# Norm handovers of a two-layer trunk formed in PSUM, squares on ScalarE, weight splits on GpSimd

## Chip, cores and metric

The kernel runs on one core of a Trainium2 chip, as one launch. The metric is the device time of that launch in microseconds (us), the median of several runs. Matmuls run on TensorE (PE in the profile; its weight loads are PEld), elementwise work on VectorE (DVE), ScalarE (ACT) and GpSimd (POOL). SP only issues transfers. SBUF is the working memory, PSUM the eight banks of 128 x 512 float32 into which matmuls write.

## What is computed

512 tokens of 1024 float32 channels pass through two layers. Each layer has a mixer and a feed-forward network, and each of the four sub-layers is normalised on both sides:

```python
def rms_norm(x, g):
    return x * lax.rsqrt(jnp.mean(x * x, axis=-1, keepdims=True) + 1e-6) * g

def swiglu_ffn(h, w_ffn_in, w_ffn_out):
    g, u = jnp.split(h @ w_ffn_in, 2, axis=-1)
    return (jax.nn.silu(g) * u) @ w_ffn_out

def conformer_conv_module(h, w_pw1, b_pw1, w_dw, b_dw, ln_g, ln_b, w_pw2, b_pw2):
    a, g = jnp.split(h @ w_pw1 + b_pw1, 2, axis=-1)
    u = a * jax.nn.sigmoid(g)
    u = causal_depthwise_conv(u, w_dw) + b_dw
    u = jax.nn.silu(layer_norm(u, ln_g, ln_b))
    return u @ w_pw2 + b_pw2

for layer in range(2):
    u = rms_norm(h, norm_mix_pre[layer])
    m = shortconv_fox_mixer(u, ...) if layer == 0 else conformer_conv_module(u, ...)
    h = h + rms_norm(m, norm_mix_post[layer])
    f = swiglu_ffn(rms_norm(h, norm_ffn_pre[layer]), ...)
    h = h + rms_norm(f, norm_ffn_post[layer])
```

The convolution module, with 31 taps, is the mixer of layer 1. The mixer of layer 0 joins a gated three-tap convolution and an eight-head causal attention with a forget-gate bias, and projects both back to 1024 channels. The feed-forward network is 2816 wide.

## The kernel before

**Layout.** Channels lie on the 128 partitions and tokens on the free axis, so the stream is eight tiles `hin[k]` of 128 x 512. Tokens are worked on in two halves of 256 (`HT`). Every float32 product is three matmul passes over operands split as v = H + L (H is v rounded to float32r, L = v - H): `mm3`, L188 to L193.

**Weights** come as one stream of 512 KB chunks in the order of use (`ensure`, L154 to L176). SP's queue loads a chunk into one of two buffers `wr`, ScalarE copies it to H (L173), and one subtraction of 128 x 1024 makes L (L175). The strings `SPLIT1` to `SPLIT4` say which chunks' subtraction goes to GpSimd; all chunks of the feed-forward input matrix (`fi`) are on VectorE.

**Handovers.** Between two sub-layers stands a handover, called a crossing (`cross`, L756). There are three: crossing 0 (attention to the feed-forward of layer 0, 236 to 290 us of the span), crossing 1 (to the convolution mixer, 615 to 685) and crossing 2 (to the feed-forward of layer 1, 840 to 892). The end of the kernel is half of one (from 1234 us). The class `Boundary` does each in these steps, per token half:

- `evict` (L638): a finished 128 x 256 or x 512 product is squared (ScalarE, L241) and copied out (L651), or added to an earlier part (VectorE, L645). The squares are added up on GpSimd, the last of the eight on VectorE (L234).
- `post0`: TensorE sums the partitions with ones (L256, a PSUM tile of its own), and VectorE turns the sums into 1/sqrt by three Newton steps on columns of two values (L276 to L291) in SBUF.
- `post1` (L655): TensorE spreads the columns over all partitions (L298). Then for each of the eight channel tiles k, VectorE forms t = s[k] * gpost * spread (L663, SBUF, two buffers), adds it to `hin[k]` in place (L672), ScalarE makes the rounded X = gpre * h (L674), VectorE its rest (L675), and GpSimd squares h (L247) and adds the squares up (L234, the last one on VectorE).
- `pre0`, `pre1`: the same statistics for the norm ahead of the next product; the spread result is copied to R (L683), which scales the next product's outputs.

TensorE's order is the program's own (a manual schedule); the other engines' orders come from a scheduler, which also places every wait. In a crossing TensorE runs the last rows of the old product for half 1, then `quads`: four rows of the new product over one half, first its eight k with rounded X (a unit of 8 matmuls each), then its eight k with the rest (4 matmuls each). The statistics are inserted after so many units (`POST0`, `POST1`, `AP0`, `AP1`, `BP0`, `BP1`, `LATE0`, `LATE1`), so TensorE stops at an insertion whose inputs are late.

**The convolution mixer.** Each channel tile's u (`glu`, L957) goes through memory into four token phases (`phases_of`), its taps are spread into blocks (`bands_of`, L881, L878, on GpSimd, VectorE or ScalarE by `BUILD`), TensorE applies them, and VectorE does the remaining taps (L918). The parts of this that need no u (the split of the last tile's taps, `picks`, the load of `bands`) stand ahead of crossing 1 in the program, and each tile's blocks are built as soon as the scheduler finds room.

**End.** Without a next norm, `post1` forms t into two sets of SBUF tiles and adds it to `hin[k]` (L668; in half 1 four of the eight on GpSimd), and the output leaves by pairs of tiles (L670).

Of the kernel before, what the change touches and what calls it, by code (L numbers as in the profile page):

```python
# [59 lines left out]
POOL_POST = (0, 1, 3, 5)  # L60
# [4 lines left out]
SPLIT4 = 'PDPPPDDD'  # L65
PAD = TAPS - 1
# [5 lines left out]
# columns of the packed per-channel vectors  # L72
# [15 lines left out]
def trunk(tc, x, vec, bands, w_xa, w_in, w_v, w_f, w_out, w_fi, w_fo, w_p1, w_p2, out):  # L88
    """Feature-major trunk: channels on partitions, tokens on the free axis.

    Every float32 product is carried by three float32r passes over operands
    split as v = H + L (H: v rounded to float32r, L = v - H).
    """
# [7 lines left out]
    with tc.tile_pool(name="sb", bufs=1) as sb, tc.tile_pool(  # L101
# [15 lines left out]
        # ---- weights: one stream of 512 KB chunks, split into H and L ahead of use  # L117
# [31 lines left out]
        pool_split = {(n, i) for n, w in (("p1", SPLIT1), ("p2", SPLIT2), ("in", SPLIT3), ("out", SPLIT4)) for i, c in enumerate(w) if c == "P"}  # L149
# [4 lines left out]
        def ensure(n, pieces=1):  # L154
            """Load and split chunks up to number n; the first chunks after a norm have their own room."""
            while len(split) < min(n, len(chunks)):
# [12 lines left out]
                for i in range(pieces):  # L169
# [4 lines left out]
                    eng = nc.gpsimd if (name, count[name]) in pool_split else nc.vector  # L174
                    eng.tensor_tensor(out=l[:, cs], in0=raw[:, cs], in1=h[:, cs], op=ALU.subtract)  # L175
# [19 lines left out]
        # ---- constants  # L195
# [12 lines left out]
        # ---- per-token statistics: sums over channels as columns, one per block of 128 tokens  # L208
        class Sums:
            """Sums over channels of a list of channel tiles, per token half, as columns:  # L210
            the tiles are added up elementwise, then ones contract the partitions."""
# [12 lines left out]
            def room(self, hf, pool=False):  # L224
                if self.n[hf] == 0:
                    return self.acc[:, hf * HT : (hf + 1) * HT]
                return alloc("sqp" if pool else "sq", (P, HT), F32, 2)

            def put(self, hf, t, last, eng=None):
                """t: [128, 256], one channel tile of the half hf."""  # L230
                if self.n[hf]:
                    acc = self.acc[:, hf * HT : (hf + 1) * HT]
                    eng = nc.vector if last else eng or nc.gpsimd
                    eng.tensor_tensor(out=acc, in0=acc, in1=t, op=ALU.add)  # L234
# [4 lines left out]
            def square(self, hf, src, last, eng=None, **extra):  # L239
                t = self.room(hf)  # L240
                act(t, src, AF.Square, **extra)  # L241
                self.put(hf, t, last, eng)

            def square_pool(self, hf, src, last):
                """As square, off the scalar engine."""
                t = self.room(hf, True)
                nc.gpsimd.tensor_tensor(out=t, in0=src, in1=src, op=ALU.mult)  # L247
                self.put(hf, t, last)

            def cols(self, hf, tag="p"):  # L250
                ps = psum(tag, (P, 2))
# [7 lines left out]
        def weave(units, inserts=()):  # L259
            """Run a generator of tensor-engine work, calling each (n, f) of inserts after n units."""  # L260
# [11 lines left out]
        def newton(a, minus_half_a, n):  # L272
            """[128, n] columns a -> 1 / sqrt(a)."""
            y = alloc("st_y", (P, 4), F32, 3)[:, :n]
            u = alloc("st_u", (P, 4), F32, 3)[:, :n]
            ts(out=y.bitcast(I32), in0=a.bitcast(I32), scalar1=-0.5, scalar2=float(0x5F3759DF),  # L276
               op0=ALU.mult, op1=ALU.add)
            for _ in range(3):
                for j in range(n):
                    js = slice(j, j + 1)  # L280
                    stt(out=u[:, js], in0=y[:, js], scalar=minus_half_a[:, js], in1=y[:, js],  # L281
                        op0=ALU.mult, op1=ALU.mult)
                stt(out=y, in0=u, scalar=1.5, in1=y, op0=ALU.add, op1=ALU.mult)
            return y
# [580 lines left out]
        def bands_of(i):  # L865
# [3 lines left out]
            if i % 2:  # L869
                big = alloc("pth", (P, 2560), F32), alloc("ptl", (P, 2560), F32)  # L870
# [310 lines left out]
```

## Time and profile before

| | us |
|---|---|
| median of 3 runs (1251.49 to 1252.73) | 1251.75 |
| span of the profiled execution, first to last instruction | 1248.6 |
| TensorE busy in the span | 1185.8 (95%) |
| VectorE busy | 735.6 (59%) |
| ScalarE busy | 490.0 (39%) |
| GpSimd busy | 265.0 (21%) |
| mean granted TensorE clock | 0.978 of full speed |

The span is what the trace shows of one execution; that execution's own device time is not recorded beside it, so the median of the runs stands for it, and 3.15 us of it lie outside the span. "Busy" counts instructions of that engine only; a share over the whole span averages stages with different limits, so the stages are read one by one below.

### The profile page before, as it was taken

The numbers are of one execution on the slowest core, as the hardware profiler recorded it, in microseconds if no ns is written. First come the engines' busy times: TensorE is split into PE (matmuls) and PEld (weight loads), VectorE is DVE, ScalarE is ACT, GpSimd is POOL, SyncE is SP. The second block draws the span as 40 slices with busy tenths as digits, with TensorE's granted clock in tenths as the row PEclk, the third lists the DMA queues.
The fourth block names the chain that finished last, engine by engine and source line by source line (L and its number), as shares of the span: only waits on it lengthen the run. The fifth ranks groups of instructions, "written<-read, shape, count | busy, mean of one in ns | idle before, by whom it ended". The sixth has DMA issues, their size and how long they took to land.

```text
span 1248.6 us, 15995 instructions
## 1 busy us (share of the span) xinstructions
PE 1185.8 (95%) x6134; PEld 1005.8 (81%) x6134; DVE 735.6 (59%) x1266; ACT 490.0 (39%) x862; POOL 265.0 (21%) x268
## 2 busy tenths in 40 slices
PE   8899999989999999999988998898999999999996
PEld 6677677888888888888887897898888888888885
DVE  7578985496443234443398999948844422444425
ACT  4366664534332222332244575464332322332220
POOL 4132322460000000001475359124300000000021
PEclk9999999999999999999989999898999999999998
DMA  5332223313233233223221543123133233233212
GB/s 177 113 106 85 85 68 102 119 51 99 89 100 102 87 99 101 94 92 102 92 71 52 168 131 97 28 68 102 51 101 101 88 98 99 89 101 102 90 46 68
DMA packets 43116, 115.86 MB, mean 93 GB/s; under 512 B 4696, under 2 KB 14040, under 8 KB 43040
## 3 DMA queue, kind: packets, MB, share of 16 engines
q1 hardware_dynamic: 39936, 109.30, 28.1%
q10 hardware_dynamic: 2384, 3.15, 0.8%
q0 software_dynamic: 720, 2.39, 0.6%
q8 instruction: 48, 0.79, 0.3%
q14 instruction: 28, 0.23, 0.1%
HBM read 109.05 MB, written 5.78 MB: 92 GB/s over the span
## 4 chain that ended last, share of the span: by engine, by line
PE 73%; DVE 17%; DMA 4%; ACT 2%; issue 2%; POOL 1%; SPq 0%; ACTq 0%; DVEq 0%; POOLq 0%
PE pg L191 22%; PE pg L193 22%; PE pg L192 22%; DVE xl L675 2%; DVE h L672 2%; DVE wl L175 2%; DVE tb L663 2%; PE pg L737 1%; DVE st_u L281 1%; POOL acc L234 1%; PE ps L298 1%; PE pg L734 1%; DMA wr<-w_fi 1%; PE pg L735 1%; PE pp L541 1%
## 5 line engine op out<-in xcount | busy, mean ns | idle before, releaser
L191 PE MATMUL pg<-xh,wh 128*128 128x512 f32 (+1 forms) x960 | 372.1, 388 | 0.2 <-DVE z L459 0.2
L193 PE MATMUL pg<-xh,wl 128*128 128x512 f32 (+1 forms) x960 | 368.4, 384 | 2.0 <-DVE wl L175 2.0
L192 PE MATMUL pg<-xl,wh 128*128 128x512 f32 (+1 forms) x960 | 367.8, 383 | 2.0 <-DVE xl L331 2.0
L173 ACT ACTIVATE wh<-wr 128x1024 fp32r<-128x1024 f32 (+1 forms) x186 | 193.3, 1040 | 424.3 <-PE pg L192 349.9
L175 DVE TENSOR_TENSOR wl<-wr,wh 128x1024 fp32r<-128x1024 f32 (+1 forms) x157 | 192.3, 1226 | 168.2 <-ACT wh L173 168.1
L234 POOL TENSOR_TENSOR acc<-acc,sq 128x256 f32<-128x256 f32 x70 | 63.7, 925 | 749.5 <-ACT sq L241 746.5
L193 PEld LDWEIGHTS pg<-xh,wl 128*128 128x128 f32 x960 | 181.1, 189 | 38.8 <-DVE wl L175 3.0
L192 PEld LDWEIGHTS pg<-xl,wh 128*128 128x128 f32 x960 | 181.4, 189 | 36.6 <-DVE xl L331 2.8
L191 PEld LDWEIGHTS pg<-xh,wh 128*128 128x128 f32 x960 | 181.6, 189 | 33.9 <-issue 0.7
L191 PE MATMUL pg<-z,wh 128*128 128x512 f32 (+1 forms) x514 | 183.2, 357 | 0.0
L192 PE MATMUL pg<-z,wh 128*128 128x512 f32 (+1 forms) x514 | 182.1, 354 | 1.1 <-DVE z L391 1.1
L193 PE MATMUL pg<-z,wl 128*128 128x512 f32 (+1 forms) x514 | 182.1, 354 | 0.0
L192 PEld LDWEIGHTS pg<-z,wh 128*128 128x128 f32 x514 | 97.9, 190 | 15.9 <-DVE z L391 1.5
L191 PEld LDWEIGHTS pg<-z,wh 128*128 128x128 f32 x514 | 97.9, 190 | 14.7 <-ACT m L651 0.3
L193 PEld LDWEIGHTS pg<-z,wl 128*128 128x128 f32 x514 | 97.9, 190 | 14.4
L785 DVE TENSOR_TENSOR t<-pg,R 128x512 f32<-128x512 f32 (+1 forms) x48 | 31.0, 645 | 126.9 <-PE pg L193 126.7
L175 POOL TENSOR_TENSOR wl<-wr,wh 128x1024 fp32r<-128x1024 f32 x29 | 71.8, 2476 | 125.4 <-ACT wh L173 113.8
L783 DVE TENSOR_TENSOR t<-pg,R 128x512 f32<-128x512 f32 (+1 forms) x48 | 31.0, 646 | 86.7 <-PE pg L193 83.0
L918 DVE SCALAR_TENSOR_TENSOR ps<-z,vecs,ps 128x512 f32<-128x512 f32 x69 | 47.7, 747 | 0.1
L674 ACT ACTIVATE xh<-h,vecs 128x256 fp32r<-128x256 f32 x48 | 23.4, 506 | 58.4 <-DVE h L672 58.4
L734 PE MATMUL pg<-xh,wh 128*128 128x256 f32 x160 | 44.9, 305 | 1.2 <-ACT xh L1082 1.2
L735 PE MATMUL pg<-xh,wl 128*128 128x256 f32 x160 | 44.3, 301 | 0.0
(250 smaller groups left out, 1526.2 us busy)
## 6 DMA issues: line engine op xcount, KB each, us to landing
wr<-w_fi SPq DMA_DIRECT2D x88, 512.0 KB
wr<-w_fo SPq DMA_DIRECT2D x44, 512.0 KB
wr<-w_p SPq DMA_DIRECT2D x24, 512.0 KB
wr<-w_in SPq DMA_DIRECT2D x16, 512.0 KB
wr<-w_out SPq DMA_DIRECT2D x8, 512.0 KB
h<-x SPq DMA_DIRECT2D x8, 256.0 KB
wr<-w_xa SPq DMA_DIRECT2D x8, 256.0 KB
wr<-w_v SPq DMA_DIRECT2D x4, 512.0 KB
```

The costliest lines, as they stand in the source:

```text
L173: act(h[:, cs], raw[:, cs], AF.Copy)
L175: eng.tensor_tensor(out=l[:, cs], in0=raw[:, cs], in1=h[:, cs], op=ALU.subtract)
L191: mm(ps, wh, xh, start=first, stop=False)
L192: mm(ps, wh, xl, start=False, stop=False)
L193: mm(ps, wl, xh, start=False, stop=last)
L234: eng.tensor_tensor(out=acc, in0=acc, in1=t, op=ALU.add)
L663: stt(out=t, in0=self.s[k][:, cs], scalar=col(self.gpost + k), in1=rp, op0=ALU.mult, op1=ALU.mult)
L734: mm(ps, wh, xt[0][k][:, cs], start=k == 0 and m % 2 == 0, stop=False)
L735: mm(ps, wl, xt[0][k][:, cs], start=False, stop=False)
L783: tt(out=tg, in0=pg, in1=R[:, cs], op=ALU.mult)
L785: tt(out=tu, in0=pu, in1=R[:, cs], op=ALU.mult)
L918: stt(out=a if j < n - 1 else res, in0=u[:, j : j + T], scalar=w_col(i, j), in1=a, op0=ALU.mult, op1=ALU.add)
```

## The change

Two new PSUM uses are the core. A `Boundary` takes four PSUM banks for its whole life: bank 0 (tag p) for the columns, the Newton work and the spread of both halves, bank 1 (tag o) for t in its lower half and the last square in its upper half, banks 2 and 3 (tag s) for the new stream tile hp, two channel tiles to a bank. The stream tile is written back to `hin[k]` by ScalarE. The squares of the norm ahead move from GpSimd to ScalarE. The first eight `fi` chunks of each layer are split on GpSimd, and every GpSimd split is cut into pieces of 128 x 256. The preparation of the convolution's taps is queued, on each engine, behind the evaluation of the second `glu` tile. At the end all eight additions are on VectorE.

```diff
-POOL_POST = (0, 1, 3, 5)
+SPLIT5 = ('PPPPPPPP' + 'D' * 36) * 2
...
+        pool_split = {... ("out", SPLIT4), ("fi", SPLIT5)) ...}
...
-                    eng = nc.gpsimd if (name, count[name]) in pool_split else nc.vector
-                    eng.tensor_tensor(out=l[:, cs], in0=raw[:, cs], in1=h[:, cs], op=ALU.subtract)
+                    if (name, count[name]) not in pool_split:
+                        tt(out=l[:, cs], in0=raw[:, cs], in1=h[:, cs], op=ALU.subtract)
+                        continue
+                    for c in range(i * D // pieces, (i + 1) * D // pieces, HT):
+                        nc.gpsimd.tensor_tensor(out=l[:, c : c + HT], in0=raw[:, c : c + HT], in1=h[:, c : c + HT],
+                                                op=ALU.subtract)
...
+            def square(self, hf, src, last, eng=None, room=None, **extra):
+                t = self.room(hf) if room is None else room
                 act(t, src, AF.Square, **extra)
                 self.put(hf, t, last, eng)
-            def square_pool(self, hf, src, last):
...
+            for s in range(3):
+                for js in each_slice(n):
+                        ts(out=u[:, js], in0=y[:, js], scalar1=y[:, js], scalar2=minus_half_a[:, js],
+                           op0=ALU.mult, op1=ALU.mult)
+                for js in each_slice(n):
+                    ts(out=(res if s == 2 else y)[:, js], in0=u[:, js], scalar1=1.5, scalar2=y[:, js],
+                       op0=ALU.add, op1=ALU.mult)
...
+            def bank(self, i):
+                if self.banks is None:
+                    self.banks = [psum(t) for t in ("po" if self.gpre is None else "poss")]
+                return self.banks[i]
+            def half(self, hf):
+                return self.bank(0)[:, hf * HT : (hf + 1) * HT]
...
-                        self.sums.square(c // HT, src[...], m == NK - 1, **extra)
+                        self.sums.square(c // HT, src[...], m == NK - 1,
+                                         room=self.bank(1)[:, HT:] if m == NK - 1 else None, **extra)
...
+            def stats(self, sums, hf):
+                r = self.half(hf)
+                self.cols[hf] = rsqrt_cols(sums.cols(hf, ps=r[:, :2]), 2, 1.0 / D, RMS_EPS, r[:, 2:8])
...
-                rp = spread(*each(self.cols[hf], 2))[:, :HT]
+                rp = spread(*each(self.cols[hf], 2), ps=self.half(hf))
                 for k in range(NK):
-                    t = alloc("t", bufs=3)[:, :HT] if self.gpre is None and k % 2 else alloc("tb", (P, HT), F32, 2)
+                    t = self.bank(1)[:, :HT]
                     stt(out=t, in0=self.s[k][:, cs], scalar=col(self.gpost + k), in1=rp, op0=ALU.mult, op1=ALU.mult)
                     if self.gpre is None:
-                        eng = nc.gpsimd if hf and k in POOL_POST else nc.vector
-                        eng.tensor_tensor(out=o[:, k % 2], in0=hin[k][:, cs], in1=t, op=ALU.add)
+                        tt(out=o[:, k % 2], in0=hin[k][:, cs], in1=t, op=ALU.add)
                     else:
-                        tt(out=hin[k][:, cs], in0=hin[k][:, cs], in1=t, op=ALU.add)
-                        act(self.x[0][k][:, cs], hin[k][:, cs], AF.Copy, scale=g)
-                        stt(out=self.x[1][k][:, cs], in0=hin[k][:, cs], scalar=g, in1=self.x[0][k][:, cs], ...)
-                        self.pre.square_pool(hf, hin[k][:, cs], k == NK - 1)
+                        i = hf * NK + k
+                        hp = self.bank(2 + i // 2 % 2)[:, i % 2 * HT : (i % 2 + 1) * HT]
+                        tt(out=hp, in0=hin[k][:, cs], in1=t, op=ALU.add)
+                        act(self.x[0][k][:, cs], hp, AF.Copy, scale=g)
+                        stt(out=self.x[1][k][:, cs], in0=hp, scalar=g, in1=self.x[0][k][:, cs], ...)
+                        self.pre.square(hf, hp, k == NK - 1, room=self.bank(1)[:, HT:] if k == NK - 1 else None)
+                        act(hin[k][:, cs], hp, AF.Copy)
...
+        def prepare():
+            room = slot(16, (P, Q + 2 * LAST_TAPS), FR)
+            band = slot(17, (P, bands.shape[1]), F32)
+            nc.gpsimd.dma_start(band, bands)
+            act(wsh, wlast, AF.Copy)
+            nc.vector.tensor_reduce(out=picks, in_=ident.rearrange("p (q c) -> p c q", q=4), axis=AX.X, op=ALU.add)
+            tt(out=wsl, in0=wlast, in1=wsh, op=ALU.subtract)
...
-                if p < last:
+                if p == 0:
+                    return
+                if p == 1:
+                    with tc.issue_after(sig.ins), tc.issue_after(out.ins), tc.issue_after(bd.pre.ins):
+                        for i in range(2):
+                            phases_of(uu[i], i)
+                        prepare()
+                        for i in range(2):
+                            bands_of(i)
+                elif p < last:
                     phases_of(uu[p], p)
                     bands_of(p)
```

`bd.pre.ins` is GpSimd's last addition of squares of the norm ahead; `issue_after` fixes only the order of issue on that instruction's engine.

## Rows read from the trace of the kernel before

**Rows 1.** TensorE's own waits over the whole span: us in total, times, longest

```profile
PE pp L256 <- DVE acc L234: 12.2, 7, 3.3
PE ps L298 <- DVE st_y L283: 12.0, 8, 3.4
PE pg L734 <- ACT xh L674: 7.7, 11, 1.6
PE pp L541 <- DVE ptl L545: 4.2, 5, 1.5
PE po L560 <- DVE t L564: 1.6, 2, 1.0
```

**Rows 2.** Busy time by stretch: PE, PEld, DVE, ACT, POOL, clock, DMA share, GB/s

```profile
615.00:685.00 70.00, 57.87 (x382) 54.41 (x381) 61.67 (x122) 29.72 (x72) 45.36 (x50) 0.90 0.19 58
685.00:793.00 108.00, 102.61 (x641) 92.65 (x639) 104.79 (x154) 59.71 (x133) 64.97 (x57) 0.97 0.43 127
```

**Rows 3.** Timeline of the attention, 127 to 132 us: start, duration, [idle before]

```profile
126.90 2.74 POOL L175 TENSOR_TENSOR wl<-wr,wh 128x1024 fp32r<-128x1024 f32 x1 [8.37 <-ACT wh L173]
...
128.08 2.12 DVE L566 TENSOR_TENSOR z<-t,z 64x512 fp32r<-64x512 f32 x1
...
131.93 0.55 PE L541 MATMUL pp<-eye,h 128*128 128x128 f32 x3 [1.19 <-DVE ptl L545]
```

**Rows 4.** Single lines: duration ns min/median/max, first and last start, forms

```profile
L663 DVE SCALAR_TENSOR_TENSOR tb<-m,vecs,ps x56: 462/473/482, 245.1 to 1243.6; 128x256 f32<-128x256 f32 x56
...
L672 DVE TENSOR_TENSOR h<-h,tb x48: 406/562/961, 245.9 to 883.0; 128x256 f32<-128x256 f32 x48
...
L645 DVE TENSOR_TENSOR m<-pg,m x14: 416/691/692, 572.2 to 1226.1; 128x512 f32<-128x512 f32 x10, 128x256 f32<-128x256 f32 x4
...
L241 ACT ACTIVATE sq<-pg x22: 364/384/406, 225.2 to 1234.9; 128x256 f32<-128x256 f32 x22
...
L458 ACT ACTIVATE z<-pg,rcol x8: 467/476/502, 63.3 to 67.5; 128x256 fp32r<-128x256 f32 x8
...
L175 DVE TENSOR_TENSOR wl<-wr,wh x157: 672/1225/2581, 5.0 to 1205.5; 128x1024 fp32r<-128x1024 f32 x149, 128x512 fp32r<-128x512 f32 x8
```

**Rows 5.** Timeline, ScalarE and VectorE in turn on one PSUM bank, 64 to 65 us

```profile
64.22 0.87 DVE L459 SCALAR_TENSOR_TENSOR z<-pg,rcol,z 128x256 fp32r<-128x256 f32 x2
...
64.73 0.48 ACT L458 ACTIVATE z<-pg,rcol 128x256 fp32r<-128x256 f32 x1 [0.24 <-DVE z L459]
```

**Rows 6.** Timeline of crossing 1: a Newton step on VectorE and three of TensorE's waits

```profile
617.23 2.21 DVE L276 TENSOR_SCALAR st_y<-st_a 128x2 int32<-128x2 int32 x1
...
623.28 1.22 PE L298 MATMUL ps<-eye,st_y 128*128 128x128 f32 x4 [2.96 <-DVE st_y L283]
...
639.02 0.58 PE L256 MATMUL pp<-ones,acc 128*128 128x1 f32 x4 [3.28 <-DVE acc L234]
...
667.20 1.22 PE L298 MATMUL ps<-eye,st_y 128*128 128x128 f32 x4 [3.37 <-DVE st_y L283]
```

**Rows 7.** Timeline of crossings 0 and 2: loop starts, a weight copy, half 1's sums

```profile
245.13 0.86 DVE L663 SCALAR_TENSOR_TENSOR tb<-m,vecs,ps 128x256 f32<-128x256 f32 x2
...
253.77 1.04 ACT L173 ACTIVATE wh<-wr 128x1024 fp32r<-128x1024 f32 x1
...
257.67 0.58 PE L256 MATMUL pp<-ones,acc 128*128 128x1 f32 x4 [0.51 <-DVE acc L234]
...
851.39 0.87 DVE L663 SCALAR_TENSOR_TENSOR tb<-m,vecs,ps 128x256 f32<-128x256 f32 x2 [2.16 <-PE ps L298]
...
861.36 0.58 PE L256 MATMUL pp<-ones,acc 128*128 128x1 f32 x4 [1.55 <-DVE acc L234]
```

**Rows 8.** Timeline of the end, 1238 to 1245 us, VectorE

```profile
1238.17 0.35 DVE L281 SCALAR_TENSOR_TENSOR st_u<-st_y,st_b 128x1 f32<-128x1 f32 x2
...
1240.03 0.48 DVE L663 SCALAR_TENSOR_TENSOR tb<-m,vecs,ps 128x256 f32<-128x256 f32 x1 [1.32 <-PE ps L298]
...
1244.73 0.41 DVE L668 TENSOR_TENSOR xl<-h,t 128x256 f32<-128x256 f32 x1
```

More of the change, by code (lines that the diff above doesn't have):

```diff
@@ L148, in trunk @@
         count = {}
-        pool_split = {(n, i) for n, w in (("p1", SPLIT1), ("p2", SPLIT2), ("in", SPLIT3), ("out", SPLIT4)) for i, c in enumerate(w) if c == "P"}
+        pool_split = {(n, i) for n, w in (("p1", SPLIT1), ("p2", SPLIT2), ("in", SPLIT3), ("out", SPLIT4),
+                                              ("fi", SPLIT5)) for i, c in enumerate(w) if c == "P"}
         split = []
@@ L233, in put @@
                     eng = nc.vector if last else eng or nc.gpsimd
-                    eng.tensor_tensor(out=acc, in0=acc, in1=t, op=ALU.add)
+                    ins = eng.tensor_tensor(out=acc, in0=acc, in1=t, op=ALU.add).ins
+                    if not last:
+                        self.ins = ins
                 elif last:
@@ L237, in put, with cols @@
                 self.n[hf] += 1
-            def square(self, hf, src, last, eng=None, **extra):
-                t = self.room(hf)
+            def square(self, hf, src, last, eng=None, room=None, **extra):
+                t = self.room(hf) if room is None else room
                 act(t, src, AF.Square, **extra)
                 self.put(hf, t, last, eng)
-            def square_pool(self, hf, src, last):
[L246 to L251, printed above, removed]
+            def cols(self, hf, tag="p", ps=None):
+                if ps is None:
+                    ps = psum(tag, (P, 2))
                 a = self.only[hf]
@@ L291, in rsqrt_cols, with spread @@
             ts(out=b, in0=sums, scalar1=-0.5 * scale, scalar2=-0.5 * eps, op0=ALU.mult, op1=ALU.add)
-            return newton(a, b, n)
-        def spread(*cols, tag="s"):
-            ps = psum(tag)
+            return newton(a, b, n, room)
+        def spread(*cols, tag="s", ps=None):
+            if ps is None:
+                ps = psum(tag)
             for j, c in enumerate(cols):
@@ L634, in __init__ @@
                 self.cols = {}
+                self.banks = None
                 if gpre is not None:
@@ L965, in glu @@
             tt(out=tg, in0=pg, in1=R[:, cs], op=ALU.mult)
[L966 removed]
+            sig = act(tg, tg, AF.Sigmoid, bias=col(V_PW1 + 8 + p))
             tt(out=ta, in0=pa, in1=R[:, cs], op=ALU.mult)
[L968 to L969 removed]
+            out = stt(out=uu[p][:, PAD + c0 : PAD + c0 + cn], in0=ta, scalar=col(V_PW1 + p), in1=tg,
+                      op0=ALU.add, op1=ALU.mult)
             if c0 + cn == T:
[L971 removed]
+                if p == 0:
[8 more added lines that the diff above has]
+                elif p < last:
                     phases_of(uu[p], p)
```

65 lines of the change are left out of this document (33 added, 32 removed).

## Prediction, made before the changed kernel was run

> **What bounds the kernel now.** TensorE is busy for 95% of the span, so I first read its own waits, then where they lie, then what the engine named was doing. It stands for 1248.6 - 1185.8 = 62.8 us. The five largest groups of its waits make 37.7 of that, and 31.9 of these belong to the norm handovers [rows 1]: 12.2 us for VectorE's last addition of squares (L234), 12.0 for a Newton result (L283), 7.7 for X (L674). The attention adds 4.2 and 1.6. By stretch, crossing 1 is the worst: TensorE works 57.9 of 70 us, at a mean granted clock of 0.90, which is another 7 us of full speed lost [rows 2]. The convolution stretch is different: VectorE is busy 104.8 of 108 us there, so work added to VectorE is paid for.
>
> VectorE is late in the handovers because its operations with SBUF data stop while GpSimd runs. In the attention a GpSimd split occupies 126.90 to 129.64; a 64x512 VectorE operation issued at 128.08 lasts 2.12 us, until just behind the split's end, and TensorE then stands 1.19 us [rows 3]. In crossing 1 a Newton operation on two columns takes 2.21 us behind such a split, and TensorE waits 2.96 [rows 6]. Operations with a PSUM operand don't show this: L663 has 462 to 482 ns over all of its 56 runs, while L672, with SBUF alone, has 406 to 961 [rows 4].
>
> **The change, part by part.**
>
> *Splits in pieces.* A piece is a quarter of the 2.74 us split, so some 0.7 us (estimate). VectorE then waits at most that in place of up to 2.4. The five and two waits in the attention, 4.2 + 1.6 us, each follow such a hold [rows 1, 3]; I take **-4** (bounds 0 and -5.8). GpSimd's splits get dearer by some 0.3 us each for the three further starts; cover is its idle time.
>
> *Splits of eight `fi` chunks off VectorE.* In crossings 0 and 2 the last addition of half 0 stands behind a 1.23 us split on VectorE (L175 [rows 4]). Without it the loop starts some 0.9 us earlier in crossing 0 and 1.5 in crossing 2 (estimates: at most the split and its queueing, at least what of the 1.23 us lies behind the last square). Each queue position that GpSimd's pieces take delays its additions by up to 0.7; nobody waits for those until the eighth.
>
> *The loop over k.* Before, VectorE was the pace. Now three kinds of wait set it. t has one buffer, so product and sum alternate: 0.47 + 0.04 + 0.42 (L663, L645 [rows 4]) = 0.93 us to the first hp. And two engines that use one PSUM bank take turns even at different columns: ScalarE's copy of a bank's second half waited for VectorE's operation on its first half, whose data it does not need, and began 0.04 us behind it, at 64.73 [rows 5]. In the program's order hp of an odd k must wait for everything done with the even k in its bank: X 0.48 (as L458), rest 0.47, square and write-back 0.38 each (L241), the sum 0.42, four handoffs of 0.04: 2.3 us. A pair costs 2.3 + 0.9 = 3.2, eight tiles 0.9 + 3 x 3.2 + 2.3 = **12.9 us**. During half 0 ScalarE also has three weight copies of 1.04 [rows 7] and three evictions of 2 x 0.38, 5.4 us; its own chain work is 8 x 1.24 = 9.9 of the 12.9, so it has 3 us free, in bits. I let 1.1 of the 5.4 land in the chain: 14 us (bounds 12.9 and 18.3). VectorE has room: 8 x 1.2 us.
>
> *New links for TensorE.* Half 1's last square goes into bank 1, where t lives, so it waits for the whole loop of half 0; then 0.38 + 0.42 and handoffs: the sums of half 1 come 14.9 us behind the loop's start. Crossing 0: 245.13 - 0.9 + 14.9 = 259.1 in place of 257.67, +1.4. Crossing 2: 851.39 - 1.5 + 14.9 = 864.8 against 861.36, +3.4 [rows 7]. In half 1 `pre0` writes bank 0 while VectorE still reads the spread there; its last read is 12.9 - 2.3 = 10.6 us into the loop, and TensorE, four or five units of X in, arrives some 2 to 3 us earlier: +2.9 and +2.0. Against that, the waits for X that lie in these two crossings, up to 7.7 us [rows 1], are absorbed by the new ones. Together **+2** (bounds -7 and +11).
>
> *Crossing 1.* The Newton wait of 2.96 goes, TensorE spreads at 620.3, the loop starts at 620.9 and lasts 1 us more, since two splits stay on VectorE: sums of half 1 at 636.8 in place of 639.02, -2.2. The next Newton wait (part of the 12.0 of [rows 1]) is worth -1.8, the one at 667.20 -3.4 [rows 6], the new `pre0` wait +2, and of the 7 us lost to the clock [rows 2] two come back as the idle time shrinks: **-7.4** (bounds -12 and -2).
>
> *Newton columns in PSUM.* Each step has four single-column operations instead of two and one of two columns. A pair takes 0.35 [rows 8], so a step grows by some 0.2 and a Newton by 0.6. Cover is TensorE's units between the insertions, except at the end.
>
> *Tap preparation.* The `bands` load, the small copy and reduction, six GpSimd blocks, one ScalarE block and two VectorE blocks move behind the second `glu`, and the first tile's phase transfers on SP's queue, with the weights behind them, start about 1 us later. TensorE reaches the first taps some 14 us after, GpSimd's three blocks need 5. VectorE's share, some 3 us, falls into its full stretch [rows 2]: **+2** (0 to +4).
>
> *The end.* No cover here. The loop was 1240.03 to 1245.14 [rows 8] with four sums on GpSimd; one buffer of t makes it 8 x 0.85 = 6.9: +1.8. The last square waits for the loop of half 0, which also grows: +0.8. The Newton: +0.6. **+3.2** (2 to 4).
>
> Sum: -4 + 2 - 7.4 + 2 + 3.2 = -4.2 us, on a span of 1248.6: 1244.4. 3.15 us lie outside the span, so **1247.5** against the median of 1251.75 (-0.34%).
>
> *PSUM operands.* VectorE's operations of the loop now read PSUM where they read SBUF. A 128x256 sum with a PSUM operand takes 416 ns at least (L645), with SBUF alone 406 (L672) [rows 4]: 10 ns apart, so I charge nothing more. The Trainium skill (VectorE: DVE Perf Modes, section "The TRN2 errata — SBUF-src ops pay a fixed extra latency per instruction") says otherwise: its table gives an operation with a PSUM source a fixed part of 120 cycles and an SBUF one 58. By it every loop would be about 1 us longer; the two rows disagree with it.
>
> **The rivals.**
> *Slower: the handovers through the banks become the bound.* Place: half 0's loop, ScalarE's queue. If its fixed order puts the weight copies and evictions into the turns, the loop takes 17 us instead of 14, and the sums of half 1 come 3 us later in three crossings: -4.2 + 9 = +4.8, **1256.5**. It decides from 15.4 us per loop on. For it: ScalarE would be busy 15 of those us. Against: VectorE and GpSimd stop holding each other up. Chance 0.25. A dearer PSUM operand gives much the same: if each costs what lies between L672's fastest run and L663's median, 473 - 406 = 67 ns [rows 4], then with four VectorE operations of a pair on the chain a loop grows by 16 x 0.067 = 1.1 us; six loops 6.4, the end 1.1: +7.5 on the forecast, **1255.0**. L645's 416 speaks against it: 0.03. The errata table named above would act in this way.
> *Much faster: the banks don't hold anyone up* and VectorE's 1.2 us per k is the pace. Loops of 10 us: 3 to 4 us off each crossing's half 0 and the 2 to 3 of the `pre0` wait, together some -17 with part caught elsewhere, -12: **1235.5**. Against it stand [rows 5]. Chance 0.13.
> *No change:* the attention's waits stay, because the fixed order of VectorE and not the hold is what makes them late: -4.2 + 4 = **1251.5**. For it: pieces hold VectorE four times. Chance 0.14.
>
> **How the numbers follow.** The forecast's own case has 0.45 and reaches from 1240 to 1252, 0.33 of it faster by over 0.2% (2.5 us, about what a measurement of this kernel can tell from no change) and 0.12 within. Faster: 0.33 + 0.13 + 0.04 of the third rival = 0.50. Within 0.2%: 0.12 + 0.05 of the first + 0.08 = 0.25. Slower: 0.20 + 0.03 + 0.02 = 0.25. The range 1238 to 1256 leaves out most of the fast rival and the upper half of the slow one, about 0.2; the likeliest case's own range is 1240 to 1252.
>
> **What would show it.** Right: no VectorE operation over 1 us in the three crossings, the waits at L298 in crossing 1 gone, TensorE's waits at the sums of half 1 and at `pre0` longer than before, L672's successor in pairs some 3.2 us apart, an end later by 3 us. Wrong: X of neighbouring k less than 1.3 us apart throughout (the fast rival), half 0 loops above 15.4 us (the slow one), or attention waits as before.

## The result and the profile after

The changed kernel takes **1288.57 us** (median of 4 runs, 1287.27 to 1289.27) against 1252.24 for the kernel before, run beside it: a ratio of 1.0285 (95% interval 1.0271 to 1.0300), 36 us slower. The forecast was 1247.5, its range 1238 to 1256. The profiled execution has a span of 1287.5 us.

The page's busy times, after:

```profile
PE 1190.8 (92%) x6134; PEld 1009.6 (78%) x6134; DVE 700.6 (54%) x1296; ACT 518.1 (40%) x958; POOL 291.7 (23%) x373
```

TensorE is busy 5 us longer, at a mean granted clock of 0.964 instead of 0.978, and idle for 96.7 us instead of 62.8. VectorE has lost 35 us of work; it was not what was short. TensorE's own waits (us in total, times, longest):

```profile
PE pp L258 <- DVE acc L239: 29.9, 6, 11.0
PE pp L315 <- DVE st_y L298: 9.6, 5, 4.1
PE pp L258 <- DVE po L696: 8.8, 3, 4.0
PE pg L770 <- ACT m L680: 8.4, 1, 8.4
PE pg L770 <- ACT xh L708: 7.7, 11, 1.3
```

Against [rows 1], the wait for the last addition of squares has grown from 12.2 to 29.9 us with fewer cases. Two groups are new: TensorE's sums wait for `po`, which is the product of the loop that reads the spread (L696), and the first unit of the new product waits 8.4 us for an *eviction* (`m`, L680). The waits for X are the same 7.7 us, eleven times. The Newton wait has become smaller, not small. The attention's groups (L541, L560 before) are down to three cases of 0.3 us. TensorE also waits 3.8 us for GpSimd at taps of the convolution (770.15 us), where it did not wait before.

Both traces hold the same 6134 matmuls in the same order, so the same one can be read in both. Where it starts, and by how much the changed kernel lags:

| matmul | before | after | lag |
|---|---|---|---|
| last wait of the attention gone | 188.46 | 184.08 | -4.4 |
| first unit of crossing 0 | 252.73 | 258.13 | +5.4 |
| last spread of crossing 0 | 293.29 | 305.04 | +11.8 |
| sums of half 1, crossing 1 | 639.02 | 654.51 | +15.5 |
| last spread of crossing 1 | 680.90 | 695.22 | +14.3 |
| ahead of crossing 2 | 837.49 | 854.58 | +17.1 |
| sums of half 1, crossing 2 | 861.36 | 889.25 | +27.9 |
| last spread of crossing 2 | 897.73 | 929.44 | +31.7 |
| last spread of the end | 1238.77 | 1274.93 | +36.2 |
| end of the span | 1248.6 | 1287.5 | +38.9 |

A negative lag means that the changed kernel is ahead. Differences between the lags at the ends of the stretches give the account: attention -4.4, crossing 0 +16.2, crossing 1 +2.5, convolution +2.8, crossing 2 +14.6, end +7.2.

One pair of channel tiles of the loop, from the timeline of crossing 0 after:

```profile
245.46 0.43 DVE L706 TENSOR_TENSOR ps<-h,po 128x256 f32<-128x256 f32 x1
...
245.92 0.48 ACT L708 ACTIVATE xh<-ps,vecs 128x256 fp32r<-128x256 f32 x1 [0.17 <-DVE ps L706]
...
246.58 0.48 DVE L709 SCALAR_TENSOR_TENSOR xl<-ps,vecs,xh 128x256 fp32r<-128x256 f32 x1
...
247.15 0.38 ACT L248 ACTIVATE sq<-ps 128x256 f32<-128x256 f32 x1
247.43 0.38 ACT L712 ACTIVATE h<-ps 128x256 f32<-128x256 f32 x1
...
247.84 0.43 DVE L706 TENSOR_TENSOR ps<-h,po 128x256 f32<-128x256 f32 x1 [0.79 <-ACT h L712]
...
248.83 0.43 DVE L706 TENSOR_TENSOR ps<-h,po 128x256 f32<-128x256 f32 x1
```

Sum, X, rest, square and write-back of an even tile follow one another, and only then may the odd tile's sum enter the bank, 2.38 us later; with the 0.99 to the next bank a pair takes 3.37. In the loops of half 1 a pair takes more, 1.37 + 2.50 = 3.87 from sum to sum, because there VectorE forms the rest of the odd tile (277.19) ahead of the next bank's sum:

```profile
276.21 0.43 DVE L706 TENSOR_TENSOR ps<-h,po 128x256 f32<-128x256 f32 x1 [0.78 <-ACT h L712]
...
277.19 0.48 DVE L709 SCALAR_TENSOR_TENSOR xl<-ps,vecs,xh 128x256 fp32r<-128x256 f32 x1
277.58 0.42 DVE L706 TENSOR_TENSOR ps<-h,po 128x256 f32<-128x256 f32 x1
...
280.09 0.43 DVE L706 TENSOR_TENSOR ps<-h,po 128x256 f32<-128x256 f32 x1 [0.79 <-ACT h L712]
```

On the turns in one bank, the Trainium skill (PSUM — Partial Sum Buffer, section "PSUM bank collisions raise a hardware error") says that two engines must not be in one bank and quadrant at once, reads included, even at other addresses; the turns in these rows agree.

Crossing 0 again, where ScalarE comes to the evictions of half 1:

```profile
256.87 0.37 ACT L248 ACTIVATE po<-ps 128x256 f32<-128x256 f32 x1 [0.55 <-DVE xl L709]
...
257.41 0.39 ACT L248 ACTIVATE sq<-pg 128x256 f32<-128x256 f32 x1
257.67 0.41 ACT L680 ACTIVATE m<-pg 128x256 f32<-128x256 f32 x1
...
258.13 0.58 PE L770 MATMUL pg<-xh,wh 128*128 128x256 f32 x1 [8.43 <-ACT m L680]
...
258.66 0.37 ACT L248 ACTIVATE po<-pg 128x256 f32<-128x256 f32 x1
```

At 256.87 the loop squares its last tile. Only behind it come three finished products (`pg`), which held the banks that TensorE needed; TensorE stood 8.43 us for the first of them. In the kernel before, ScalarE takes the same three at 247.65, 250.48 and 252.52, all ahead of the fifth X of the loop:

```profile
250.48 0.36 ACT L241 ACTIVATE sq<-pg 128x256 f32<-128x256 f32 x1
250.74 0.38 ACT L651 ACTIVATE m<-pg 128x256 f32<-128x256 f32 x1
...
253.35 0.51 ACT L674 ACTIVATE xh<-h,vecs 128x256 fp32r<-128x256 f32 x1 [0.17 <-DVE h L672]
```

In crossings 1 and 2 the last two evictions stand behind the squares of the seventh and the eighth tile; before, they stood ahead of the sixth X in crossing 1, and the last one ahead of the fourth in crossing 2. In crossing 2 this shows as late sums:

```profile
884.61 0.47 ACT L248 ACTIVATE sq<-pg,vecs 128x256 f32<-128x256 f32 x1
...
888.22 0.45 ACT L248 ACTIVATE po<-pg,vecs 128x256 f32<-128x256 f32 x1 [0.27 <-DVE acc L239]
...
889.25 1.01 PE L258 MATMUL pp<-ones,acc 128*128 128x1 f32 x4 [10.98 <-DVE acc L239]
```

### The profile page after: what moved, and what is told of

Read it like the earlier page. It is cut to its first block, busy times and chain, and to the rows that moved or that the text cites. A ratio compares the mean times of both kernels' runs of the same rounds, so it can differ in the third digit from the quotient of the medians.

```text
span 1287.5 us, 16342 instructions
## 1 busy us (share of the span) xinstructions
PE 1190.8 (92%) x6134; PEld 1009.6 (78%) x6134; DVE 700.6 (54%) x1296; ACT 518.1 (40%) x958; POOL 291.7 (23%) x373
## 4 chain that ended last, share of the span: by engine, by line
PE 65%; DVE 8%; ACT 3%; DMA 1%; issue 1%; POOL 1%; ACTq 0%; DVEq 0%; POOLq 0%
PE pg L196 19%; PE pg L197 19%; PE pg L198 19%; PE pg L770 2%; PE pg L771 2%; PE pg L773 1%; DVE po L696 1%; DMA wr<-w_fi 1%; PE pp L937 1%; DVE xl L709 1%; PE po L937 1%; ACT wh L174 1%; ACT sq L248 1%; POOL wl L179 1%; DVE ps L706 1%
## 5 line engine op out<-in xcount | busy, mean ns | idle before, releaser
L176 DVE TENSOR_TENSOR wl<-wr,wh 128x1024 fp32r<-128x1024 f32 (+1 forms) x145 | 175.9, 1215 | 165.9 <-ACT wh L174 165.7
L239 POOL TENSOR_TENSOR acc<-acc,sq 128x256 f32<-128x256 f32 x106 | 88.4, 846 | 774.9 <-ACT sq L248 773.7
L179 POOL TENSOR_TENSOR wl<-wr,wh 128x256 fp32r<-128x256 f32 x164 | 131.7, 833 | 140.6 <-ACT wh L174 140.5
L196 PEld LDWEIGHTS pg<-z,wh 128*128 128x128 f32 x514 | 97.8, 190 | 14.7 <-ACT m L680 0.3
L258 PE MATMUL pp<-ones,acc 128*128 128x1 f32 x64 | 11.0, 276 | 38.7 <-DVE acc L239 29.9
```

The lines of the kernel that those rows point to most:

```text
L176: tt(out=l[:, cs], in0=raw[:, cs], in1=h[:, cs], op=ALU.subtract)
L179: nc.gpsimd.tensor_tensor(out=l[:, c : c + HT], in0=raw[:, c : c + HT], in1=h[:, c : c + HT], op=ALU.subtract)
L196: mm(ps, wh, xh, start=first, stop=False)
L239: ins = eng.tensor_tensor(out=acc, in0=acc, in1=t, op=ALU.add).ins
```

## The experiments

The kernel before, run beside each group, had medians of 1252.2 to 1253.8 us; ratios are to it.

**First: single parts.** u1: `room=None` for the last square of a finished product.

```diff
-    self.sums.square(..., room=self.bank(1)[:, HT:] if m == NK - 1 else None, **extra)
+    self.sums.square(..., **extra)
```

> The changed kernel with the last square of each finished product back in an SBUF tile of its own instead of the upper half of bank 1. Theory (bank links): in half 1 that square waits for the whole loop of half 0, and with it the sums of half 1 and the evictions queued behind it on ScalarE. Undone, the sums of half 1 wait only for VectorE's last read of the spread in bank 0, some 10 us earlier in crossing 0 and 5 to 6 us in crossings 1 and 2: 1266 to 1272 us. Rival (ScalarE's fixed order: the evictions of rows 6 and 7 stand behind most of the loop's work on that queue whatever the bank does): 1282 to 1289 us, with the three long waits of 8 to 11 us still there.

1288.46 us (1.0268, 1.0241 to 1.0295): nothing. The link that the prediction had priced is not the one that holds; whatever the bank does, the evictions stand late in ScalarE's order (the wait for one is 8.7 us here). The waits for the last addition shrink from 29.9 to 24.2 us, but this does not reach the end.

u2: t in SBUF.

```diff
-    t = self.bank(1)[:, :HT]
+    t = alloc("tb", (P, HT), F32, 2)
```

> The changed kernel with t in two SBUF tiles as before, the stream tile still in PSUM. The upper half of bank 1 is still shared by the last squares of both halves, so the link stays. Theory (bank links): product and sum no longer alternate, a pair costs 2.9 instead of 3.4 us, the loops of half 0 end 1.5 to 2 us earlier: 1282 to 1285 us. Rival (t is the link that counts): the sums of half 1 come 5 us or more earlier in each crossing, 1270 to 1276 us.

1278.94 us (1.0195, 1.0170 to 1.0221): 9.6 us, more than the theory and less than the rival. By matmul starts it is spread out: 1.7 to 2.4 us at the waits behind each half-1 loop and 2.1 at the end, hence shorter loops, while the long waits stay (28.7 us in 6 cases for L239, 9.7 for the eviction).

u3: the Newton steps on SBUF columns.

```diff
-    rsqrt_cols(sums.cols(hf, ps=r[:, :2]), 2, 1.0 / D, RMS_EPS, r[:, 2:8])
+    rsqrt_cols(sums.cols(hf, ps=r[:, :2]), 2, 1.0 / D, RMS_EPS)
```

> The changed kernel with the Newton steps on SBUF columns as before (one two-column operation in place of two). Theory: a Newton takes 4.0 us in PSUM and should take about 2.4 in SBUF; TensorE stands behind it in five places and at the end, so 1280 to 1284 us. Rival (GpSimd's splits hold the SBUF columns as before and eat the gain): 1286 to 1290 us, with single Newton operations above 0.7 us.

1287.59 us (1.0264, 1.0239 to 1.0289): 1 us, which is not told apart from none; the rival's number, but not by its mechanism. The waits do shrink by 1.5, 3.0 and 2.0 us in three places, and 1.4 us come back at each of two others.

b1: the kernel before with two parts of the change.

```diff
+SPLIT5 = ('PPPPPPPP' + 'D' * 36) * 2
...
+    for c in range(..., HT):
+        nc.gpsimd.tensor_tensor(out=l[:, c : c + HT], ...)
```

> The kernel before with two parts of the change alone: GpSimd's splits in pieces of 128 x 256, and the first eight chunks of the feed-forward input matrix split on GpSimd. Theory: the attention gives its 4.6 us, crossing 1 another 2 to 5 where a Newton operation stood behind a whole split: 1242 to 1246 us. Rival (the pieces delay GpSimd's own additions of squares, which it alone makes in the loops): the crossings lose what the attention gains, 1250 to 1254 us.

1263.60 us (1.0078, 1.0052 to 1.0104). Theory and rival both missed it: the attention gives 3.7 us, but GpSimd's queue holds the sums of half 0 far more than a piece. The timeline of its crossing 0:

```profile
231.73 2.82 POOL L179 TENSOR_TENSOR ptl<-wr,pth 128x256 fp32r<-128x256 f32 x4
...
234.50 0.73 POOL L239 TENSOR_TENSOR acc<-acc,sq 128x256 f32<-128x256 f32 x1
...
235.69 2.77 POOL L179 TENSOR_TENSOR wl<-wr,wh 128x256 fp32r<-128x256 f32 x4 [0.46 <-ACT wh L174]
...
238.41 0.73 POOL L239 TENSOR_TENSOR acc<-acc,sq 128x256 f32<-128x256 f32 x1
239.17 0.43 DVE L239 TENSOR_TENSOR acc<-acc,sq 128x256 f32<-128x256 f32 x1 [12.17 <-POOL acc L239]
239.65 0.59 PE L261 MATMUL pp<-ones,acc 128*128 128x1 f32 x2 [6.27 <-DVE acc L239]
```

An addition waits for all four pieces of a split, which stand together in the queue: pieces shorten what VectorE is held for, not what GpSimd's own queue is.

**Second: the order, and which splits.** u4: the loop of half 0 is queued in portions, one behind each later eviction. The first two lines stand at the end of `evict`; `some` queues the given channel tiles.

```diff
+    if self.owed:
+        self.owed.pop(0)()
...
-    for k in range(NK):
...
+    if hf or self.gpre is None:
+        some(range(NK))
+    else:
+        some((0, 1))
+        self.owed = [lambda k=k: some((k, k + 1)) for k in (2, 4, 6)]
```

> The changed kernel with one thing moved: of the loop of half 0 only the first two channel tiles are queued at its start; each later pair is queued behind the next eviction of half 1, so that on ScalarE the evictions stand ahead of it. Theory (ScalarE's order: evictions of rows 6 and 7 stand behind most of the loop's work, and TensorE then has no PSUM bank free in crossing 0 and late sums in all three): the wait of 8.4 us in crossing 0 goes, the waits for half 1's sums shrink by 3 to 5 us in crossings 1 and 2: 1268 to 1276 us. Rival (the length of the loop itself sets the end, in whatever order): the waits move to the sums of half 1, 1283 to 1290 us.

1278.60 us (1.0201, 1.0168 to 1.0234): 10 us, and the wait of 8.43 is gone. Between the two ranges, nearer the theory's. The largest group that stays is TensorE's sums behind the loop's last read of the spread in bank 0:

```profile
PE pp L258 <- DVE po L705: 22.3, 6, 6.4
```

u5 sets `SPLIT5 = 'D' * 88`: the feed-forward splits go back to VectorE.

> The changed kernel with the splits of the feed-forward input matrix back on VectorE, whole; GpSimd's other splits stay in pieces. Theory (GpSimd's queue is the cost: eight splits of 2.8 us stand among the additions of squares): crossings 0 and 2 lose 4 to 6 us each of their delay, 1276 to 1282 us. Rival (the splits lengthen VectorE's loops by as much as they free GpSimd): 1286 to 1291 us.

1294.52 us (1.0333, 1.0301 to 1.0365): 6 us slower, 3.5 above the rival's range. In the changed kernel these splits lie better on GpSimd. b2 is b1 without `SPLIT5`; b3 has pieces for the matrices `in` and `out` alone:

```diff
+    if name not in ("in", "out"):
+        nc.gpsimd.tensor_tensor(out=l[:, cs], in0=raw[:, cs], in1=h[:, cs], op=ALU.subtract)
+        continue
```

> The kernel before with its GpSimd splits in pieces and nothing else. Theory (the loss of the pieces with the splits of the feed-forward input matrix comes from the latter in crossings 0 and 2, 12 us; the attention's gain of 3.7 is the pieces'): 1249 to 1252 us, with 3 to 4 us more in the convolution where pieces stand between the blocks on GpSimd's queue. Rival (pieces cost as much as they give): 1254 to 1258 us.

> The kernel before with pieces for the splits of layer 0's mixer alone (the matrices in and out); the convolution's splits stay whole. Theory: the attention's gain without the convolution's loss, 1247 to 1249 us, faster than before. Rival (the pieces lengthen GpSimd's queue ahead of crossing 0 as well): no gain, 1252 to 1255 us.

b2: 1250.28 us (0.9968, 0.9950 to 0.9986), b3: 1247.55 (0.9955, 0.9937 to 0.9973). Both as the theory had it. By matmul starts the attention gives 3.7 and 4.7 us. So in the kernel before the pieces alone are a gain, and the feed-forward splits on GpSimd, added to them, cost 13 us (b1 less b2).

**Third: the banks.** u6 builds on u4:

```diff
-    return self.bank(0)[:, hf * HT : (hf + 1) * HT]
+    return self.bank(hf)[:, :HT]
...
-    t = self.bank(1)[:, :HT]
+    t = alloc("tb", (P, HT), F32, 2)
...
-    ... room=self.bank(1)[:, HT:] if ... == NK - 1 else None
```

> The kernel of u4_staged with the other bank sharing removed too: each token half has its columns, Newton work and spread in a bank of its own (half 0 in bank 0, half 1 in bank 1), t lies in two SBUF tiles, the last squares in SBUF. The stream tile stays in PSUM. In u4_staged TensorE's sums still wait in six places for VectorE's last read of the spread in bank 0, 3.7 + 4.0 + 6.4 + 2.4 + 3.4 + 2.4 = 22.4 us. Theory (the shared bank 0 is the second cost): these waits go, 4 to 8 of the 22 us come back as waits for the squares or for X: 1258 to 1266 us. Rival (the squares' sums are as late by themselves, and the bank is only the last of several releasers): 1270 to 1279 us.

1259.99 us (1.0057, 1.0036 to 1.0077): 18.6 us less than u4, the theory. What came back is the wait for X, 13.9 us in 14 cases instead of 10.6 in 11. u7 adds the Newton on SBUF (as u3) and the end of the kernel before:

> The kernel of u6_banks_apart with the Newton steps on SBUF columns and the end as before (four of the last eight additions on GpSimd, t in two sets of tiles). Theory (the Newton in PSUM costs 1.6 us each, TensorE stands behind it in some four places, and the end's loop 2.7): 6 to 10 us less than u6_banks_apart. Rival (other waits end at the same time, as u3_newton_sbuf's 1 us against 1288.6 suggests): 2 to 4 us less.

1256.36 us (1.0034, 1.0018 to 1.0049): 3.6 us less than u6, at the rival's upper edge, though the two intervals overlap. u8 calls `prepare()` where its lines stood before and drops the `issue_after` block:

> The changed kernel with the tap preparation where it was before (ahead of crossing 1 in the program, each tile's blocks as soon as there is room). Theory (the queueing behind the second tile makes the first blocks late on GpSimd: TensorE's wait of 3.8 us at the first taps): that wait goes, 1284 to 1286 us. Rival (GpSimd's splits in pieces stand ahead of the blocks wherever they are queued, as in the kernel before with the pieces and the feed-forward splits, which waited 2.8 us more there without this move): 1288 to 1290 us.

1290.43 us (1.0300, 1.0276 to 1.0325): not faster. The wait of 3.8 us, which lies at the taps of 770.15 and not at the first ones (709.38, on time), shrinks to 2.1 us in three cases, and the gain is lost at later waits. No cost of queueing the preparation later is shown. u9 takes the stream out of PSUM, and with it t and the last squares (as in u2 and u1, not printed again):

```diff
-    hp = self.bank(2 + i // 2 % 2)[:, i % 2 * HT : (i % 2 + 1) * HT]
+    hp = hin[k][:, cs]
...
-    act(hin[k][:, cs], hp, AF.Copy)
```

> The changed kernel with the stream formed in place in SBUF as before (no hp, no write-back on ScalarE), t in two SBUF tiles, the last squares in SBUF; squares on ScalarE, the splits, the shared bank 0 and the Newton steps stay. Theory (the loop is long because sum, X, rest, square and write-back take turns in the stream's bank: 3.4 us a pair): a pair costs 2.8 us, the loops of half 0 end 3 to 5 us earlier, and with them the evictions and sums behind them: 1268 to 1276 us. Rival (VectorE's SBUF operations are now held by GpSimd's 0.7 us pieces, which fill GpSimd in crossings 0 and 2): 1280 to 1290 us, with single additions of 0.7 us and more.

1271.93 us (1.0153, 1.0136 to 1.0170): 16.7 us less than the changed kernel, the theory, and 7 less than u2, which has t in SBUF alone, although the eviction wait of crossing 0 grows to 11.7.

**Fourth: what is left.** u11 is u6 without the portions. u10 is u7 with `SPLIT5 = 'D' * 88`. u12 is u10 with u9's stream. b4 is b3 with `self.pre.square` (ScalarE) for `square_pool`, and four tiles for the squares in place of two for each engine.

> The changed kernel with the banks apart as in u6_banks_apart, but the loop of half 0 queued in one piece as in the change. Theory (two separate costs): the waits of TensorE for bank 0 go (4.0 + 2.4 + 2.4 us) and t in SBUF gives its 10 us, but the evictions still stand behind the loop on ScalarE, so the wait of 8 us in crossing 0 and late sums in crossings 1 and 2 stay: 1266 to 1273 us. Rival (bank sharing alone is the cause, the order only its consequence): 1258 to 1263 us, as u6_banks_apart.

> The kernel of u7_newton_end with the splits of the feed-forward input matrix back on VectorE, whole. Theory (GpSimd's splits stand among the additions of squares at the start of crossings 0 and 2, as in the kernel before with them, where they cost 12 us): 1248 to 1252 us. Rival (with squares on ScalarE GpSimd has the room, and the splits are better there than among VectorE's loop): 1256 to 1262 us.

> The kernel of u10_no_fi_apart with the stream tile formed in place in SBUF as before, without the write-back. What is left of the change is then: pieces, squares on ScalarE, tap preparation, the order of the loop, a bank for each half. Theory (the stream's bank is a cost of its own: sum, X, rest, square and write-back in turns, 3.4 us a pair): 4 to 8 us below u10_no_fi_apart. Rival (once the order is right the loop is not what TensorE waits for): within 2 us of u10_no_fi_apart.

> The kernel of b3_pieces_layer0 (before, with pieces in layer 0's mixer alone) with the squares of the norm ahead on ScalarE instead of GpSimd. Theory (GpSimd's squares hold VectorE's SBUF additions in the loops, ScalarE has room for 0.4 us more per tile): 1 to 4 us below b3_pieces_layer0's 1247.6, 1243.5 to 1246.5 us. Rival (the squares delay the X and the evictions on ScalarE's queue): 1248 to 1254 us.

u11: 1277.50 us (1.0201, 1.0181 to 1.0222). Neither: banks apart give 11 us alone (nearly all of it t in SBUF, as u2) and 18.6 once the order is right, because until then the evictions are later than the bank (TensorE's wait for one is still 11.0 us in u11). u10: 1260.33 (1.0057, 1.0036 to 1.0078), the rival: 4 us worse than u7, the same way as u5, though the intervals of u10 and u7 overlap. u12: **1233.01** (0.9834, 0.9812 to 0.9856), 27 us below u10, far beyond the theory, and 20 below the kernel before. TensorE's waits for X in u10 and u12:

```profile
PE pg L787 <- ACT xh L719: 16.8, 14, 2.0
```

```profile
PE pg L785 <- ACT xh L718: 3.2, 7, 1.1
```

These explain half of the 27 us. TensorE's idle time falls from 69.7 us in u10 to 53.2 in u12, 13.6 of it at X, and its busy time from 1189.6 to 1179.6, at a mean granted clock of 0.984 instead of 0.973.

b4: 1253.01 (1.0006, 0.9993 to 1.0019), the rival, and the most telling miss. With nothing in PSUM that was not there before, two waits of the changed kernel appear:

```profile
PE pp L263 <- DVE acc L241: 27.3, 6, 10.8
PE pg L741 <- ACT m L658: 7.5, 1, 7.5
```

In crossing 0 ScalarE turns to the finished products behind the square of the eighth tile, as in the changed kernel; in b3 they are done ahead of the fifth X, as before:

```profile
254.28 0.51 ACT L681 ACTIVATE xh<-h,vecs 128x256 fp32r<-128x256 f32 x1
...
255.00 0.64 ACT L248 ACTIVATE sq<-pg 128x256 f32<-128x256 f32 x2
```

So it is the squares on ScalarE that move the evictions behind the loop, not the banks. u13 and u14 undo one part of u12 each: the portions (`if hf or self.gpre is None:` becomes `if True:`), and the squares, which go back to GpSimd.

> The kernel of u12_stream_sbuf_apart with the loop of half 0 queued in one piece again. Theory (the order counts by itself: ScalarE's evictions of half 1 stand behind the loop's X and squares): 1243 to 1252 us, with TensorE short of banks in crossing 0 again. Rival (the order cost time only because the stream's bank made the loop long): 1232 to 1238 us.

> The kernel of u12_stream_sbuf_apart with the squares of the norm ahead on GpSimd as before. Theory (the squares on ScalarE are the useful part of the change: GpSimd's squares hold VectorE's SBUF operations in the loop): 1240 to 1248 us, with single additions in the loop of 0.8 us and more. Rival (order and banks make the gain): 1231 to 1237 us.

u13: 1252.03 us (0.9990, 0.9977 to 1.0003), u14: 1241.81 (0.9911, 0.9884 to 0.9938): the theory in both. The order is worth 19 us and the squares on ScalarE 9, given the order.

The loop by itself, from the start of its first X to the start of its last (us; crossings 0, 1 and 2):

| kernel | half 0 | half 1 |
|---|---|---|
| before | 13.3, 14.3, 12.9 | 10.8, 9.9, 10.8 |
| changed | 13.1, 16.4, 17.6 | 13.8, 13.8, 13.8 |
| u6, t in SBUF | 16.8, 16.7, 17.0 | 12.5, 12.3, 12.3 |
| u9, stream in SBUF too | 11.1, 11.9, 11.6 | 8.7, 8.7, 8.7 |
| u14, squares on GpSimd | 13.2, 12.4, 11.7 | 10.8, 11.2, 10.8 |

Half 1 has no evictions and no weight copies in its loop; there the chain through the banks shows by itself: 3 to 4 us longer than before, where the loop with t and the stream in SBUF (u9) is 1 to 2 us shorter.

## Why the prediction was wrong, step by step

One reading went wrong without consequence: TensorE's fourth largest wait is 4.6 us for a Newton result at 39.03 us, which [rows 1] leaves out, so the five largest groups make 40.7 us and not 37.7. No term of the sum rests on it.

*Attention, -4*: right. -4.4 by the matmul starts, and b2 and b3 show the pieces as the cause. The 0.3 us that a split was to get dearer did not show: four pieces take 2.77 to 2.82 us in b1, a whole split 2.74 [rows 3].

*VectorE is freed from GpSimd*: right, and worth less than it cost. L706 and L709 (L672 and L675 before) no longer vary [rows 4]:

```profile
L706 DVE TENSOR_TENSOR ps<-h,po x48: 416/429/430, 242.3 to 911.5; 128x256 f32<-128x256 f32 x48
...
L709 DVE SCALAR_TENSOR_TENSOR xl<-ps,vecs,xh x48: 472/484/486, 243.3 to 912.6; 128x256 fp32r<-128x256 f32 x48
```

*The loop, 12.9 us of chain, 14 in half 0*: the turns inside a bank were sized rightly (2.38 to 2.50 us for the forecast 2.3), the step to the next bank was not where VectorE's order disturbs it (0.99 to 1.37 for 0.9). So the chain of half 1, from the first product to the last sum, takes 14.7 us for 12.9. In half 0 it takes 14.0 in crossing 0, as forecast, but 17.4 and 19.6 in crossings 1 and 2. The slow rival named the right place, ScalarE's fixed order, and loops of 17 us, but not the mechanism: it put the evictions into the turns, and they came behind them. The delay is largest in crossing 0, whose loop is no longer than forecast. The other fault is what the sum did with 12.9: beyond the `pre0` waits, half 1's loop was never set against the one before, which has 10 to 10.8 from first to last X, against 13.8 now.

*"During half 0 ScalarE also has ... three evictions"; "I let 1.1 of the 5.4 land in the chain"*: **this is the step that failed.** The sum took the evictions to stand between the turns and asked only how much they lengthen the loop. It did not ask who waits for an eviction that stands behind the loop in ScalarE's queue: TensorE, whose banks they hold (8.4 us in crossing 0), and the sums of half 1 (9.9 and 11.0 us in crossings 1 and 2). None of the three evictions of crossing 0 lengthened its loop. u4 shows 10 us of this in the changed kernel, u13 19 us in the version without the other faults, and b4 that the squares on ScalarE cause it.

*Half 1's last square through bank 1, +1.4 and +3.4*: the right place and the wrong cause. From the spread of half 0 to the sums of half 1 the lag grows by 10 us in crossing 0 and by 13 in crossing 2, but u1, which removes the link, leaves the time as it was; the eviction is late by ScalarE's order.

*`pre0` behind the reads of the spread, +2.9, +2.0, +2*: right in kind and a little low, 4.0, 2.4 and 2.4 us. That half 1's sums stand behind the same reads in bank 0 was not seen; it shows once the order is mended (u4: 22.3 us in all, u6: gone).

*Waits for X "are absorbed by the new ones"*: wrong, 7.7 us before and after. Of those after, eight lie at the loops of half 1, at 3.9 us a pair, and three at the long loop of half 0 in crossing 2.

*Crossing 1, -7.4*: +2.5. The Newton wait of 2.96 [rows 6] fell to 1.25 and the one of 3.37 is gone, as forecast, but the sums of half 1 wait 9.9 us instead of 3.28. The 2 us expected back from the clock did not come: it was 0.88 from 627 to 699 us, against 0.90 [rows 2].

*Newton, +0.6*: about +2.3 where nothing covers it (sums to spread at the end: 2.77 us before, 5.08 after). The step grew from 0.58 to 1.18: its two pairs of column operations take 0.61 and 0.50 us, where the forecast had 0.35 [rows 8] for each.

```profile
L292 DVE TENSOR_SCALAR pp<-pp,st_b x84: 281/289/293, 236.8 to 1274.2; 128x1 f32<-128x1 f32 x84
```

```profile
L281 DVE SCALAR_TENSOR_TENSOR st_u<-st_y,st_b x108: 198/215/2439, 39.1 to 1238.3; 128x1 f32<-128x1 f32 x108
```

L292 (after) takes 74 ns more than L281 (before), but it is not shown that PSUM is the reason, for the operation changed too: L292 has two column scalars, L281 one. L298, with one, takes 231 ns in PSUM and 218 with its result in SBUF. The operation that is the same in both kernels, the first guess of the Newton steps, takes 168 ns in SBUF (L276, before) and in PSUM (L284, after):

```profile
L298 DVE TENSOR_SCALAR st_y<-pp x28: 211/218/225, 239.8 to 1274.7; 128x1 f32<-128x1 f32 x28
```

```profile
L276 DVE TENSOR_SCALAR st_y<-st_a x18: 154/168/2215, 38.8 to 1236.8; 128x2 int32<-128x2 int32 x18
```

```profile
L284 DVE TENSOR_SCALAR pp<-pp x14: 160/168/169, 236.6 to 1271.3; 128x2 int32<-128x2 int32 x14
```

By these rows a PSUM operand by itself costs 0 to 13 ns, so the prediction lost little by charging nothing for it. What it missed is the price of the new form, most likely of the second column scalar and of two single columns in place of one operation on both; that was not tried by itself. The Trainium skill (VectorE: DVE Perf Modes, section "The TRN2 errata — SBUF-src ops pay a fixed extra latency per instruction") has 62 cycles more for a PSUM source, an estimated 65 ns at the page's 0.96 GHz; neither these rows nor the 128x256 sums show it (429 ns with PSUM after, 417 in u12 with SBUF).

*Tap preparation, +2*: not shown. The first taps are on time and later ones wait 3.8 us, but u8 puts the preparation back and is no faster. The convolution stretch is 2.8 us longer all the same; b2 is 2.7 slower than b3, which differs by the pieces of that stretch's splits, so these are the likely cause, but the two intervals overlap.

*The end, +3.2*: +7.2, in the forecast's three parts: sums 2.0 (0.8), Newton 2.3 (0.6), loop and output 2.7 (1.8). The loop alternates as expected:

```profile
1276.19 0.49 DVE L696 SCALAR_TENSOR_TENSOR po<-m,vecs,pp 128x256 f32<-128x256 f32 x1 [1.31 <-PE pp L315]
1276.71 0.42 DVE L700 TENSOR_TENSOR xl<-h,po 128x256 f32<-128x256 f32 x1
1277.17 0.49 DVE L696 SCALAR_TENSOR_TENSOR po<-m,vecs,pp 128x256 f32<-128x256 f32 x1
```

*Feed-forward splits*: forecast as a small gain. In the kernel before they cost 13 us on GpSimd (b1), in the changed one they save 6 there (u5; 4 in u10, within the noise). What decides is most likely what else GpSimd has: before, the squares too. That was not tried by itself.

Taken one after the other, the undone parts account for 32 of the 36 us: order 10.0, banks and t 18.6, Newton and end 3.6 (1288.6 to 1256.4). The stream in PSUM, 27 us (u10 to u12), lies beyond that: it is what kept the good parts, squares on ScalarE and pieces, from paying. Open is why the scheduler puts the evictions behind the loop once the squares are on ScalarE.

## What to carry to other kernels

When work moves to an in-order queue, look for what it can push back in that queue and who waits for it: here a few squares of 0.4 us delayed evictions, and TensorE stood 8 to 11 us for banks and sums. A value in PSUM that two engines use in turn costs the sum of all their operations and handoffs per bank (here 3.4 to 3.9 us for two tiles, against 2.5 in SBUF, u9); set that chain against the loop that it replaces, in every stretch. Undo the parts in combination too: here the undos of single parts gave -6 to 10 us (u5 and u4), and their combination with the new order 56 (u12).

## What the runs showed that was not expected

The same part changes sign with its surroundings: squares on ScalarE are worth 9 us with the loop queued in portions (u14 against u12) and cost 5 us without (b4 against b3). Splits of the feed-forward matrix on GpSimd cost 13 us in one kernel and save 6 in the other. And a column operation of VectorE with two column scalars in PSUM takes 289 ns where one with a single column scalar in SBUF takes 215, though the same two-column operation takes 168 ns in either memory.
